# How a two-layer mixer trunk begins its first layer: four column blocks over four row tiles instead of three over six

## The chip, the cores and the metric

The kernel runs on one core of a Trainium2 chip. The metric is the device time of one execution in microseconds (us). TensorE is called PE here, its weight loads PEld, VectorE DVE, ScalarE ACT, GpSimd POOL and SyncE SP.

## What is computed

Two layers of a residual stream x of 256 rows and 2048 channels. Each layer normalizes x, projects it by one wide matrix, runs a convolution branch and a latent-attention branch on parts of the projection, merges both by gates, projects the result and adds it to x. Cut to the part that matters here:

```python
def hybrid_layer(x, ...):
    h = rmsnorm(x, norm_g)
    proj = h @ w_in                      # 2048 x 13376
    (c_a, c_glu, c_gate, q_down, kv_down, k_pe, m_gate,
     g_conv, g_mla) = jnp.split(proj, idx, axis=-1)
    y_conv = conv_branch(c_a, c_glu, c_gate, ...) @ w_proj_conv
    y_mla = mla_branch(q_down, kv_down, k_pe, m_gate, cos, sin, ...) @ w_proj_mla
    y = jax.nn.sigmoid(g_conv) * y_conv + jax.nn.sigmoid(g_mla) * y_mla
    return x + y @ w_out
```

The convolution's input is `c_a * sigmoid(c_glu)`. q_down, kv_down and k_pe, 512 + 512 + 64 columns, are the narrow ("down") projections from which queries, keys and values are made.

## The kernel before, in words

**Products.** Every matrix product is done in float32 accuracy from two halves. A weight w is split into hi (w rounded to PE's fp32r type, by an ACT cast) and lo = w - hi (by a DVE subtraction); the activations likewise into h_hi and h_lo. Three products are summed in PSUM: h_hi x hi, h_lo x hi and h_hi x lo. The stationary operand is a 128 x 128 tile of the activations, the weights move past it.

**Pieces.** Weights come from HBM in pieces: two K tiles (row tiles of 128 channels) of one block of n columns (512, 384 or 320), so 128 x 2n numbers. A piece needs 12 products: 2 K tiles x 2 row blocks of 128 rows (t = 0, 1) x 3 halves. Eight pieces make one block of a 2048-channel product. Pieces are numbered in the order in which PE takes them; "piece 10" below is the eleventh. For each piece, SP issues the load (`load`), ACT casts hi (`split_hi`), DVE subtracts lo (`split_lo`), and PE multiplies. SP loads 4 pieces ahead of the cast, the cast is issued 3 pieces ahead of PE and the subtraction 2 (`LOAD_AHEAD`, `HI_AHEAD`, `LO_AHEAD`). There are 5 raw buffers, 4 for hi, 3 for lo; a load waits for the lo of the piece 5 before it.

**Order.** On each engine instructions run in the order in which the program issues them (`InOrder`), so a wait holds up all that stands behind it. `background` counts slots, one after each piece, and at each slot issues steps that are due (`at_slot`): evacuations of PSUM, loads, the steps of other parts of the layer.

**The first layer's begin.** x arrives transposed, K tile by K tile (`load_x`; tile 0 comes with the gains in `gx`). `first_h` makes h_hi and h_lo of one K tile, on ACT (tile 0: DVE) and DVE. It stands just before the cast of the first piece that reads those K tiles (`h_of`). The rows of x are loaded again untransposed (`xres`) to sum their squares on ACT (`first_sums`, `sum_x`); the factor `rinv_x` that normalizes rows is first needed when a block is evacuated. So that PE does not need a new K tile with every piece, `plan_first` (line 211) and `products_together` (line 419) take several blocks together: here the first gated unit ("unit 0", 512 columns, `glu`) and the first two down blocks of 384 columns, over the first 3 pieces (6 K tiles) each, by turns; after that the rest of unit 0 (5 pieces), of down block 0 and of down block 1. Down block 2, of 320 columns, follows by itself (`product`, line 385), then `down_after` (line 692) starts the steps for the keys and queries. The blocks that are open at the same time stand in different PSUM homes: `acc0`, `acc1`, `s`, `tp`.

**The very first piece** is loaded, cast and subtracted by K tile, and not as a whole (`SINGLE = 1`, lines 258 and 268), and its products run K tile by K tile. Ahead of them `N_WARM = 19` products on zeros (line 580) warm PE while the loads come. The loads at the start are written out by hand:

```python
    act.dma_start(gx, g_in)
    load_x(act, 1, 2)
    ...
    load(0)
    load(1)
    load(2)
    load_x(sp, 2, 4)
    load(3)
    load(4)
    load_x(sp, 4, 6)
    at_slot(1, lambda: load_x(sp, 6, 8))
    at_slot(3, lambda: load_x(sp, 8, 12))
    at_slot(5, lambda: load_x(sp, 12, 16))
```

Of the kernel before, what the change touches and what calls it, by code (L numbers as in the profile page):

```python
# [57 lines left out]
R_QA, R_KVA, R_QR, R_KR, R_N = 0, LORA, 2 * LORA, 2 * LORA + ROPE, 2 * LORA + 2 * ROPE  # L58

KS = 2  # L60
SINGLE = 1
FIRST_TOGETHER, FIRST_DOWNS = 3, (2, 1)
TOGETHER = (("pconv", 0), ("wout", 0))
N_WARM = 19

# [64 lines left out]
def trunk(ctx: ExitStack, tc: tile.TileContext, xT, x, g_in, pos, win, wuq, wukv, wpc, wpm, wo, cst, rows, invf, out):  # L132
# [78 lines left out]
    def plan_first(layer, stream):  # L211

        ap, nk = streams[stream]
        count, groups = 1 + FIRST_DOWNS[layer], nk // KS
        widths = blocks_of_layer()[stream][:count]
        starts = [nk * P * sum(widths[:i]) for i in range(count)]
        if layer == 0:
            joint, rest = range(FIRST_TOGETHER), range(FIRST_TOGETHER, groups)
            order = [(i, g) for g in joint for i in range(count)] + [(i, g) for i in range(count) for g in rest]
        else:  # L220
            order = [(i, g) for part in (range(6), range(6, groups)) for i in range(count) for g in part]
        mine = []
        for i, g in order:
            n = widths[i]
            size = P * KS * n
            at = starts[i] + g * size
            pieces.append((ap[layer, at : at + size].rearrange("(p e) -> p e", p=P), n))
            mine.append((i, g, len(pieces) - 1))
            if i == 0 and layer == 0:
                h_of[len(pieces) - 1] = range(g * KS, (g + 1) * KS)  # L230
        taken[layer, stream] = (count, nk * P * sum(widths))
        return nk, widths, mine
# [20 lines left out]
    def load(i):  # L253
        if i >= len(pieces) or i in loaded:
            return
        ap, n = pieces[i]
        loaded[i] = t = raw_p.tile([P, KS * n], F32, tag="raw", name=f"raw{i}")
        for a in range(0, KS, 1 if i < SINGLE else KS):
            k = slice(a, a + 1 if i < SINGLE else KS)
            sp.dma_start(part_of(i, t, k), part_of(i, ap, k))  # L260

    def split_hi(i):
        if i >= len(pieces) or i in highs:
            return
        load(i)
        highs[i] = split_p.tile([P, KS * pieces[i][1]], F32R, tag="hi", name=f"hi{i}", bufs=4)
        singly = i < SINGLE
        for a in range(0, KS, 1 if singly else KS):
            k = slice(a, a + 1 if singly else KS)

            for step in ("h", "w"):
                if step == "w":
                    act.copy(part_of(i, highs[i], k), part_of(i, loaded[i], k))
                    if singly:
                        split_lo(i, k)
                else:
                    for c in h_of.get(i, ())[k.start : k.stop]:
                        first_h(c)
        for a in range(1, LOAD_AHEAD + 1):
            load(i + a)  # L280

# [69 lines left out]
    def order_of_products(i, last):  # L351

        two = range(2)
        if i < SINGLE:
            return [(t, kk, p) for kk in range(KS) for p in range(3) for t in two]
        high, low = (lambda t, p: [(t, kk, p) for kk in range(KS)]), (lambda t: [(t, kk, 2) for kk in range(KS)])
        if last:
            return high(0, 0) + high(0, 1) + high(1, 0) + low(0) + high(1, 1) + low(1)  # L360
        return [e for t in two for p in two for e in high(t, p)] + low(0) + low(1)
# [54 lines left out]
                steps.insert(0, (clock[0] + 1 + evac_at, costs, evac))  # L416
            background(n)

    def products_together(planned, stat, evacuate, evac_at, costs, before=None):

        nk, widths, mine = planned
        pts = []
        for i in range(2):
            blocks_begun[0] += 1
            tags = [f"acc{blocks_begun[0] % 2}{t}" for t in range(T)]
            pts.append([acc_p.tile([P, 512], F32, tag=tag, name=f"acc{mine[0][2]}_{i}{t}") for t, tag in enumerate(tags)])
        if len(evac_at) == 3:
            pts.insert(0, [s_p.tile([P, 512], F32, tag=f"s{t}", name=f"acc{mine[0][2]}_s{t}") for t in range(T)])
        if len(evac_at) == 4:
            both = tp_p.tile([P, T, 512], F32, tag="tp", name=f"acc{mine[0][2]}_tp")  # L430
            pts[1:1] = [
                [s_p.tile([P, 512], F32, tag=f"s{t}", name=f"acc{mine[0][2]}_s{t}") for t in range(T)],
                [both[:, t] for t in range(T)],
            ]
        ends = nk // KS - 1

        def evac(i):
            for t in range(T):
                evacuate(i, t, pts[i][t][:, : widths[i]])

        for i, g, piece in mine:
            n = widths[i]
            for a in range(HI_AHEAD + 1):
                split_hi(piece + a)
                if a <= LO_AHEAD:
                    split_lo(piece + a)
            hi, lo, _ = done[piece]
            if before and i == 0:
                before(g)
            for t, kk, part in order_of_products(piece, g == ends):  # L450
                k = g * KS + kk
                sh, sl = stat(k, t)
                stationary, w = ((sh, hi), (sl, hi), (sh, lo))[part]
                pe.matmul(
                    pts[i][t][:, :n], stationary, woven(piece, w, kk),
                    start=k == 0 and part == 0, stop=k == nk - 1 and part == 2,
                )
            if g == ends:
                steps.insert(0, (clock[0] + 1 + evac_at[i], costs[i] if isinstance(costs[0], tuple) else costs, lambda i=i: evac(i)))
            background(n)  # L460
# [103 lines left out]
    act.dma_start(gx, g_in)  # L564
    load_x(act, 1, 2)
    act.copy(sin2[:, 0, 0, :], ones[:, :HALF].bitcast(F32))
    load(0)
    load(1)
    load(2)
    load_x(sp, 2, 4)  # L570
    load(3)
    load(4)
    load_x(sp, 4, 6)
    at_slot(1, lambda: load_x(sp, 6, 8))
    at_slot(3, lambda: load_x(sp, 8, 12))
    at_slot(5, lambda: load_x(sp, 12, 16))


    warm = tp_p.tile([P, 256], F32, tag="tp", name="warm")
# [85 lines left out]
    for l in range(DEPTH):  # L665
# [783 lines left out]
        for kind, i, pl in planned:  # L1449
            if kind == "glu":  # L1450
                at = 0 if i in (2, 5) else EVAC_AT
                if i == 0 and l == 0:
                    at = 6 - 2 * FIRST_TOGETHER
                    for n, (t, c) in enumerate([(0, 0), (0, 2), (1, 0), (1, 2)]):
                        begin, end = first_sums(t, c)
                        at_slot((4, 5, 6, 9)[n], begin)
                        at_slot((9, 9, 10, 12)[n], end, 0.0, 1.5)
                    at_slot(13, sum_x, 2.2)
                elif i == 0:
                    at_slot(8, sum_x, 2.2)  # L1460
                if i == 0:
                    at_slot(10, load_consts)
                if i == 0:
                    if l == 0:
                        rope_table_steps()
                    downs = FIRST_DOWNS[l]
                    products_together(
                        pl, uses_h, lambda i, t, ps: down_evac(i - 1, t, ps) if i else glu_evac(0, t, ps),
                        (at,) + downs * (EVAC_AT,), ((0.9, 2.2),) + downs * ((0.0, 1.0),),
                    )  # L1470
                    continue
                product(pl, uses_h, lambda t, ps, i=i: glu_evac(i, t, ps), at, (0.9, 2.2))
            elif kind == "down":
# [26 lines left out]
            elif kind == "cgate":  # L1500
                product(pl, uses_h, lambda t, ps, i=i: cgate_evac(i, t, ps), costs=(0.0, 2.0))
            elif kind == "pconv":
                while "yc" not in keep:
                    run_fill()
                products_together(pl, stat_of(*keep["yc"]), pconv_evac, (EVAC_AT, EVAC_AT, EVAC_AT, 0), (2.4, 0.0), before_pconv)
            elif i == 0:
                wout_begin(0)
                wout_begin(1)
                products_together(pl, stat_of(*keep["y"]), wout_evac, (EVAC_AT, EVAC_AT), (1.25, 1.5))
            else:  # L1510
                at_slot(3, lambda i=i: wout_begin(i))
                product(pl, stat_of(*keep["y"]), lambda t, ps, i=i, f=wout_evac: f(i, t, ps),
                        0 if i == 3 else EVAC_AT, (1.25, 1.5),
                        final=last_half if last_layer and i == 3 else None)
# [43 lines left out]
def _layout(inp):  # L1558
# [33 lines left out]
    rows_of_w = {"wuq": _rows()[:LORA], "wukv": _rows()[:LORA]}  # L1592
    g = np.stack([f("norm_g")[l][rows_of[l]] for l in range(DEPTH)])
    win = np.stack([_blocked(f("w_in")[l][rows_of[l]][:, cols], bl["win"]) for l in range(DEPTH)])
    first = win[0, : SINGLE * P * KS * bl["win"][0]].reshape(SINGLE, P, 2, KS, -1)
    first[...] = first.transpose(0, 1, 3, 2, 4).copy().reshape(first.shape)
    return {
        "xT": np.ascontiguousarray(x.reshape(SEQ, NCT, P).transpose(2, 1, 0)),
        "x": x.reshape(T, P, D),
# [29 lines left out]
```

## Time and profile before

| | |
|---|---|
| median of 3 runs | 1785.10 us (1784.71 to 1785.26) |
| profiled execution: its own time | 1785.14 us |
| profiled execution: span of the trace | 1783.4 us |
| busy in the span: PE, PEld, DVE, ACT, POOL | 1777.9, 1572.1, 1537.7, 1293.8, 550.4 us |
| moved by DMA | 463.65 MB, mean 260 GB/s |

The span runs from the first instruction to the last. Each engine's busy time is the union of its instructions, so 100% for PE says that it had hardly any gap, not that each product was as short as it can be.

### The profile page before, as it was taken

Reading aid. Unit: us, or ns where it says so; the run is one execution under the profiler, and the core shown is the slowest. Engines: PE = TensorE matmul, PEld = TensorE weight load, DVE = VectorE, ACT = ScalarE, POOL = GpSimd, SP = SyncE. Lnnn points to the kernel's source line nnn. Section 1 sums busy time; section 2 is a strip of 40 time slices with the busy share of each in tenths; the row PEclk is TensorE's granted clock in tenths of the full one; section 3 lists DMA queues with packets and bytes.
Section 4 is the critical chain, followed back from the end, with each engine's and each line's share of the span. In section 5 each row is a group of like instructions: output and inputs, shape, how many; then the busy total and the mean of one; then the engine's idle time right before and its main releaser. Section 6 shows DMA issues by size and latency. Waiting matters only on the chain.

```text
span 1783.4 us, 27086 instructions
## 1 busy us (share of the span) xinstructions
PE 1777.9 (100%) x8577; PEld 1572.1 (88%) x8577; DVE 1537.7 (86%) x2485; ACT 1293.8 (73%) x2397; POOL 550.4 (31%) x1009
## 2 busy tenths in 40 slices
PE   9999999999999999999999999999999999999999
PEld 9988888888888888888899888888888888888887
DVE  6899899898999998867669898989999999887674
ACT  7679889888877675744567698898888777666442
POOL 0055556642311110021421555566333111100210
PEclk9999999999999999999999999999999999999999
DMA  9787888887989986678977888788879899866785
GB/s 334 242 277 256 279 268 275 273 290 235 281 247 254 268 247 231 220 245 285 314 259 229 261 286 269 255 285 275 286 238 279 244 254 262 257 210 220 247 281 179
DMA packets 149375, 463.65 MB, mean 260 GB/s; under 512 B 24816, under 2 KB 30704, under 8 KB 149232
## 3 DMA queue, kind: packets, MB, share of 16 engines
q1 hardware_dynamic: 105712, 360.42, 61.5%
q0 software_dynamic: 42928, 100.98, 20.2%
q8 instruction: 67, 1.10, 0.3%
q14 instruction: 76, 0.62, 0.1%
q10 hardware_dynamic: 592, 0.54, 0.1%
HBM read 399.18 MB, written 44.04 MB: 249 GB/s over the span
## 4 chain that ended last, share of the span: by engine, by line
PE 99%; DMA 1%; DVE 0%; ACT 0%; issue 0%; DVEq 0%; ACTq 0%
PE acc L143 90%; PE acc_s L143 4%; PE acc_tp L143 2%; PE s L143 2%; PE o_ps L143 1%; DMA raw<-in_win 1%; DVE xres L143 0%; DVE u_t L143 0%; ACT hi L143 0%; DVE qkc L143 0%; DVE su L143 0%; PE var L143 0%; ACT su L143 0%; PE mu L143 0%; DVEq L143 0%
## 5 line engine op out<-in xcount | busy, mean ns | idle before, releaser
L143 ACT CAST hi<-raw 128x1024 fp32r<-128x1024 f32 (+2 forms) x681 | 693.5, 1028 | 369.5 <-PE acc L143 229.8
L143 DVE TENSOR_TENSOR lo<-raw,hi 128x1024 fp32r<-128x1024 f32 (+2 forms) x681 | 812.0, 1195 | 144.7 <-PE acc L143 79.1
L143 PE MATMUL acc<-hi,hT 128*128 128x512 f32 (+2 forms) x1728 | 400.8, 372 | 0.2 <-DVE su L143 0.2
L143 PEld LDWEIGHTS acc<-hi,hT 128*128 128x128 f32 x1728 | 319.7, 189 | 40.9 <-PE acc L143 0.4
L143 DVE SCALAR_TENSOR_TENSOR v_t<-u_t,cst,v_t 128x256 f32<-128x256 f32 x562 | 239.9, 479 | 2.1
L143 PE MATMUL acc<-hi,h_hi 128*128 128x512 f32 (+2 forms) x832 | 241.5, 372 | 0.0
L143 PE MATMUL acc<-hi,h_lo 128*128 128x512 f32 (+2 forms) x832 | 241.5, 372 | 0.0
L143 PE MATMUL acc<-lo,hT 128*128 128x512 f32 (+2 forms) x864 | 220.1, 372 | 0.0
L143 PE MATMUL acc<-lo,h_hi 128*128 128x512 f32 (+2 forms) x832 | 211.8, 372 | 0.0
L143 PEld LDWEIGHTS acc<-lo,hT 128*128 128x128 f32 x864 | 160.8, 189 | 20.6
L143 PEld LDWEIGHTS acc<-hi,h_lo 128*128 128x128 f32 x832 | 155.5, 189 | 19.8
L143 PEld LDWEIGHTS acc<-lo,h_hi 128*128 128x128 f32 x832 | 154.8, 189 | 19.7
L143 PEld LDWEIGHTS acc<-hi,h_hi 128*128 128x128 f32 x832 | 154.6, 189 | 19.2
L143 POOL DMA_DIRECT2D turn_d<-gate x176 | 95.8, 553 | 217.6 <-DVE gate L143 151.9
L143 POOL DMA_DIRECT2D taps<-taps x71 | 62.1, 875 | 299.4 <-ACT taps L143 219.4
L143 ACT ACTIVATE taps<-u_t,cst 128x256 f32<-128x256 f32 x292 | 128.4, 498 | 2.9 <-DVE v_t L143 2.2
L143 PE MATMUL acc<-hi,oT 128*128 128x512 f32 x512 | 122.2, 379 | 0.0
L143 PE MATMUL acc<-hi,yT 128*128 128x512 f32 x512 | 122.0, 378 | 0.0
L143 POOL DMA_DIRECT2D turned<-turn_d x88 | 50.0, 578 | 217.1 <-ACT hi L143 59.9
L143 PE MATMUL acc<-hi,qkc 128*128 128x512 f32 x448 | 110.8, 380 | 0.1
L143 PEld LDWEIGHTS acc<-hi,oT 128*128 128x128 f32 x512 | 96.8, 189 | 13.7
L143 PEld LDWEIGHTS acc<-hi,yT 128*128 128x128 f32 x512 | 96.6, 189 | 13.6
(197 smaller groups left out, 2428.1 us busy)
## 6 DMA issues: line engine op xcount, KB each, us to landing
raw<-in_win SPq DMA_DIRECT2D x383, 512.0 KB, 4.6
raw<-in_wpm SPq DMA_DIRECT2D x64, 512.0 KB, 5.0
raw<-in_wpc SPq DMA_DIRECT2D x64, 512.0 KB, 4.3
raw<-in_wo SPq DMA_DIRECT2D x64, 512.0 KB, 5.2
taps<-taps POOLq DMA_DIRECT2D x71, 256.0 KB, 6.5
raw<-in_wukv SPq DMA_DIRECT2D x32, 512.0 KB, 4.4
turned<-turn_d POOLq DMA_DIRECT2D x56, 256.0 KB, 5.6
raw<-in_win SPq DMA_DIRECT2D x32, 384.0 KB, 5.1
```

The source lines that it names most:

```text
L143: ins = getattr(self.engine, name)(*a, **k)
```

## The change

Unit 0 and all three down blocks start together, over the first 2 pieces (4 K tiles) each, in the order down block 2 (320 columns), down block 0 (384), unit 0 (512), down block 1 (384). The four open blocks stand in `s` (unit 0), two `acc` homes and `tp` (down block 2). The two smallest first pieces are loaded, cast and subtracted by K tile and by turns, and their 24 products run together, K tile by K tile; piece 1 then has none left. Behind the joint part come the rest of unit 0 (6 pieces) and of each down block (6 pieces each). `down_after` is called behind the joint product. x tiles 4 to 15 are loaded at slots 2, 3, 5 and 7, where tiles 4 and 5 stood among the first loads and the others at slots 1, 3 and 5. There are 17 warming products. The second layer's parameters stay as they were.

```diff
-SINGLE = 1
-FIRST_TOGETHER, FIRST_DOWNS = 3, (2, 1)
+SINGLE = 2
+FIRST_TOGETHER, FIRST_ORDER, FIRST_DOWNS = 2, (3, 1, 0, 2), (3, 1)
-N_WARM = 19
+N_WARM = 17
...
-            order = [(i, g) for g in joint for i in range(count)] + [(i, g) for i in range(count) for g in rest]
+            order = [(i, g) for g in joint for i in FIRST_ORDER] + [(i, g) for i in range(count) for g in rest]
...
-            if i == 0 and layer == 0:
+            if layer == 0 and i == (FIRST_ORDER[0] if g in joint else 0):
                 h_of[len(pieces) - 1] = range(g * KS, (g + 1) * KS)
...
+    def load_singles():
+        for i in range(SINGLE):
+            loaded[i] = raw_p.tile([P, KS * pieces[i][1]], F32, tag="raw", name=f"raw{i}")
+        for kk in range(KS):
+            for i in range(SINGLE):
+                k = slice(kk, kk + 1)
+                sp.dma_start(part_of(i, loaded[i], k), part_of(i, pieces[i][0], k))
+
+    def split_singles():
+        for i in range(SINGLE):
+            high_tile(i)
+        for kk in range(KS):
+            k = slice(kk, kk + 1)
+            first_h(kk)
+            for i in range(SINGLE):
+                act.copy(part_of(i, highs[i], k), part_of(i, loaded[i], k))
+            for i in range(SINGLE):
+                split_lo(i, k)
...
-            for t, kk, part in order_of_products(piece, g == ends):
+            todo = [(piece, i) + e for e in order_of_products(piece, g == ends)]
+            if piece < SINGLE:
+                first = [(q, j) for j, _, q in mine[:SINGLE]]
+                todo = [(q, j, t, kk, p) for kk in range(KS) for p in range(3) for q, j in first for t in range(T)] if piece == 0 else []
+            for q, j, t, kk, part in todo:
...
-    load(0)
-    load(1)
+    load_singles()
     load(2)
+    load(3)
     load_x(sp, 2, 4)
-    load(3)
     load(4)
-    load_x(sp, 4, 6)
-    at_slot(1, lambda: load_x(sp, 6, 8))
-    at_slot(3, lambda: load_x(sp, 8, 12))
-    at_slot(5, lambda: load_x(sp, 12, 16))
+    for slot, (a, b) in ((2, (4, 6)), (3, (6, 8)), (5, (8, 12)), (7, (12, 16))):
+        at_slot(slot, lambda a=a, b=b: load_x(sp, a, b))
...
-                    at = 6 - 2 * FIRST_TOGETHER
+                    at = 6 - 3 * FIRST_TOGETHER
...
+                        homes=("acc", "acc") if l else ("s", "acc", "acc", "tp"),
                     )
+                    if downs == len(DOWN_BLOCKS):
+                        down_after()
                     continue
```

PE's first rows in the kernel before (acc_s is the home of unit 0; the numbers behind hi, lo and raw are buffer numbers, one per piece; the size is that of the output):

```order
L143 MATMUL warm<-const-float32-0.0 128x256 x19
L143 MATMUL acc_s_163<-hi_165,h_hi 128x512
L143 MATMUL acc_s_164<-hi_165,h_hi 128x512
L143 MATMUL acc_s_163<-hi_165,h_lo 128x512
L143 MATMUL acc_s_164<-hi_165,h_lo 128x512
L143 MATMUL acc_s_163<-lo_169,h_hi 128x512
```

and now (acc_3 is down block 2 in `tp`, acc_10 and acc_11 are down block 0):

```order
L143 MATMUL warm<-const-float32-0.0 128x256 x17
L143 MATMUL acc_3_163<-hi_164,h_hi 128x320 x2
L143 MATMUL acc_10_159<-hi_165,h_hi 128x384
L143 MATMUL acc_11_160<-hi_165,h_hi 128x384
L143 MATMUL acc_3_163<-hi_164,h_lo 128x320 x2
L143 MATMUL acc_10_159<-hi_165,h_lo 128x384
L143 MATMUL acc_11_160<-hi_165,h_lo 128x384
```

The first products are narrower, and each pair of one block is followed by a pair of the other, which needs a load of its own.

SP's queue in the kernel before, from the load of piece 7 (raw_212 is piece 8, raw_230 piece 9, raw_253 piece 10, raw_275 piece 11, raw_298 piece 12; the x_in row of 512 columns is x tiles 6 and 7, those of 1024 are x tiles 8 to 11 and 12 to 15):

```order
L143 DMA raw_193<-in_win 128x768
L143 DMA x_in<-in_xT 128x512
L143 DMA raw_212<-in_win 128x768
L143 DMA raw_230<-in_win 128x1024
L143 DMA x_in<-in_xT 128x1024
L143 DMA raw_253<-in_win 128x1024
L143 DMA xres<-in_x 128x512 x2
L143 DMA raw_275<-in_win 128x1024
L143 DMA x_in<-in_xT 128x1024
L143 DMA xres<-in_x 128x512 x2
L143 DMA raw_298<-in_win 128x1024
```

and now (raw_231 is piece 9, raw_250 piece 10, raw_272 piece 11, raw_299 piece 12, raw_325 piece 13; the x_in rows of 512 columns are x tiles 4 and 5, 6 and 7):

```order
L143 DMA x_in<-in_xT 128x512
L143 DMA raw_231<-in_win 128x1024
L143 DMA x_in<-in_xT 128x512
L143 DMA raw_250<-in_win 128x1024
L143 DMA xres<-in_x 128x512 x2
L143 DMA raw_272<-in_win 128x1024
L143 DMA x_in<-in_xT 128x1024
L143 DMA xres<-in_x 128x512 x2
L143 DMA raw_299<-in_win 128x1024
L143 DMA xres<-in_x 128x512 x2
L143 DMA raw_325<-in_win 128x1024
L143 DMA x_in<-in_xT 128x1024
```

x tiles 8 to 11 moved from ahead of piece 10 to behind piece 11, x tiles 12 to 15 from ahead of piece 12 to behind piece 13.

ACT's order now, from the h_hi of K tiles 8 and 9 (hi_346 is piece 10, hi_435 piece 13; junk is a square of x's rows for the sums):

```order
L143 ACTIVATE h_hi<-x_in,gx 128x256 x2
L143 CAST hi_346<-raw_250 128x1024
L143 ACTIVATE h_hi<-x_in,gx 128x256 x2
L143 CAST hi_368<-raw_272 128x1024
L143 ACTIVATE junk,ss_x<-xres 128x512 x4
L143 ACTIVATE h_hi<-x_in,gx 128x256 x2
L143 CAST hi_402<-raw_299 128x1024
L143 ACTIVATE junk,ss_x<-xres 128x512 x2
L143 ACTIVATE h_hi<-x_in,gx 128x256 x2
L143 CAST hi_435<-raw_325 128x1024
```

From piece 10 on the kinds and the order of ACT's rows are those of before (there hi_340 is piece 10 and hi_428 piece 13).

## Rows read from the trace of the kernel before

**Rows 1.** The page: busy us and shares by engine; the chain that ended last
```profile
PE 1777.9 (100%) x8577; PEld 1572.1 (88%) x8577; DVE 1537.7 (86%) x2485; ACT 1293.8 (73%) x2397; POOL 550.4 (31%) x1009
...
PE 99%; DMA 1%; DVE 0%; ACT 0%; issue 0%; DVEq 0%; ACTq 0%
```

**Rows 2.** PE's waits, whole span: waited for, us in total, times, longest
```profile
PE warm L143 <- PEq L1618: 0.8, 1, 0.8
PE acc_s L143 <- ACT hi L143: 0.3, 1, 0.3
PE acc L143 <- DVE su L143: 0.2, 1, 0.2
```

**Rows 3.** The chain in order of time: start us, us, what, instructions
```profile
8.41 3.90 PE acc L143 x24
...
25.29 12.95 PE acc_s L143 x60
```

**Rows 4.** Timeline 0 to 9 us: start, us, engine, operation, [idle before, releaser]
```profile
0.78 4.18 PE L143 MATMUL warm<-const-float32-0.0 128*128 128x256 f32 x19 [0.78 <-PEq L1618]
...
4.60 0.62 ACT L143 CAST hi<-raw 128x512 fp32r<-128x512 f32 x1 [1.41 <-DMA raw<-in_win]
...
4.78 0.35 DVE L143 TENSOR_SCALAR h_hi<-gx 128x256 fp32r<-128x256 f32 x1 [3.77 <-DMA gx<-in_g]
...
5.27 0.70 PE L143 MATMUL acc_s<-hi,h_hi 128*128 128x512 f32 x2 [0.31 <-ACT hi L143]
...
5.77 0.51 ACT L143 ACTIVATE h_hi<-x_in,gx 128x256 fp32r<-128x256 f32 x1 [0.55 <-DMA x_in<-in_xT]
...
6.84 0.70 PE L143 MATMUL acc_s<-hi,h_hi 128*128 128x512 f32 x2
7.38 0.59 PE L143 MATMUL acc_s<-hi,h_lo 128*128 128x512 f32 x2
...
8.24 0.49 PE L143 MATMUL acc<-hi,h_hi 128*128 128x384 f32 x2
```

**Rows 5.** Timeline 18 to 35 us, ACT, and SP's issue of piece 13
```profile
21.97 1.05 ACT L143 CAST hi<-raw 128x1024 fp32r<-128x1024 f32 x1 [0.88 <-DMA raw<-in_win]
...
23.48 0.33 SPq L143 DMA_DIRECT2D raw<-in_win  x1
...
24.81 1.04 ACT L143 CAST hi<-raw 128x1024 fp32r<-128x1024 f32 x1 [0.97 <-DMA raw<-in_win]
...
28.64 0.89 ACT L143 ACTIVATE h_hi<-x_in,gx 128x256 fp32r<-128x256 f32 x2
29.44 1.03 ACT L143 CAST hi<-raw 128x1024 fp32r<-128x1024 f32 x1
...
32.55 1.03 ACT L143 CAST hi<-raw 128x1024 fp32r<-128x1024 f32 x1
```

**Rows 6.** DMA issues from 23.4 to 24 us: KB each, median us to landing
```profile
raw<-in_win SPq DMA_DIRECT2D x1, 512.0 KB, 7.8
```

**Rows 7.** Stretches: length, busy us by engine, PEclk, DMA share, GB/s
```profile
4.00:8.00 4.00, 3.69 (x17) 2.71 (x17) 3.06 (x6) 2.70 (x5) 0.00 (x0) 1.00 1.00 368
16.00:19.00 3.00, 3.00 (x20) 2.97 (x19) 1.62 (x3) 1.68 (x5) 0.00 (x0) 1.00 0.95 342
19.00:22.00 3.00, 3.00 (x17) 2.71 (x16) 2.16 (x4) 1.98 (x4) 0.00 (x0) 1.00 0.95 301
22.00:38.00 16.00, 16.00 (x81) 14.42 (x80) 11.73 (x27) 14.02 (x29) 0.00 (x0) 1.00 1.04 401
```

**Rows 8.** Timeline 38 to 58 us, ACT, DVE and PE
```profile
38.35 1.28 ACT L143 ACT_TABLE_LOAD   x1 [1.19 <-DVE rinv_x L143]
...
40.94 0.95 DVE L143 TENSOR_TENSOR lo<-raw,hi 128x768 fp32r<-128x768 f32 x1
...
43.27 0.81 PE L143 MATMUL acc<-lo,h_hi 128*128 128x384 f32 x4
...
51.27 0.73 ACT L143 CAST hi<-raw 128x640 fp32r<-128x640 f32 x1 [1.07 <-PE acc L143]
```

More of the change, by code (lines that the diff above doesn't have):

```diff
@@ L257, in load, with high_tile @@
         loaded[i] = t = raw_p.tile([P, KS * n], F32, tag="raw", name=f"raw{i}")
-        for a in range(0, KS, 1 if i < SINGLE else KS):
-            k = slice(a, a + 1 if i < SINGLE else KS)
-            sp.dma_start(part_of(i, t, k), part_of(i, ap, k))
+        sp.dma_start(t, ap)
+    def load_singles():
[5 more added lines that the diff above has]
+                sp.dma_start(part_of(i, loaded[i], k), part_of(i, pieces[i][0], k))
+    def high_tile(i):
+        highs[i] = split_p.tile([P, KS * pieces[i][1]], F32R, tag="hi", name=f"hi{i}", bufs=4)
+        return highs[i]
+    def split_singles():
[8 more added lines that the diff above has]
+                split_lo(i, k)
     def split_hi(i):
@@ L265, in split_hi @@
         load(i)
[L266 to L278, printed above, removed]
+        if i < SINGLE:
+            split_singles()
+        else:
+            for c in h_of.get(i, ()):
+                first_h(c)
+            act.copy(high_tile(i), loaded[i])
         for a in range(1, LOAD_AHEAD + 1):
@@ L355, in order_of_products @@
         two = range(2)
-        if i < SINGLE:
-            return [(t, kk, p) for kk in range(KS) for p in range(3) for t in two]
         high, low = (lambda t, p: [(t, kk, p) for kk in range(KS)]), (lambda t: [(t, kk, 2) for kk in range(KS)])
@@ L417, in product, with products_together @@
             background(n)
-    def products_together(planned, stat, evacuate, evac_at, costs, before=None):
+    def products_together(planned, stat, evacuate, evac_at, costs, before=None, homes=("acc", "acc")):
         nk, widths, mine = planned
         pts = []
[L423 to L434, printed above, removed]
+        for i, home in enumerate(homes):
+            if home == "tp":
+                both = tp_p.tile([P, T, 512], F32, tag="tp", name=f"acc{mine[0][2]}_{i}")
+                pts.append([both[:, t] for t in range(T)])
+                continue
+            blocks_begun[0] += home == "acc"
+            pool, tag = (acc_p, f"acc{blocks_begun[0] % 2}") if home == "acc" else (s_p, "s")
+            pts.append([pool.tile([P, 512], F32, tag=f"{tag}{t}", name=f"acc{mine[0][2]}_{i}{t}") for t in range(T)])
         ends = nk // KS - 1
@@ L446, in products_together @@
                     split_lo(piece + a)
-            hi, lo, _ = done[piece]
             if before and i == 0:
                 before(g)
-            for t, kk, part in order_of_products(piece, g == ends):
+            todo = [(piece, i) + e for e in order_of_products(piece, g == ends)]
[3 more added lines that the diff above has]
+            for q, j, t, kk, part in todo:
                 k = g * KS + kk
                 sh, sl = stat(k, t)
-                stationary, w = ((sh, hi), (sl, hi), (sh, lo))[part]
+                stationary, w = ((sh, done[q][0]), (sl, done[q][0]), (sh, done[q][1]))[part]
                 pe.matmul(
-                    pts[i][t][:, :n], stationary, woven(piece, w, kk),
+                    pts[j][t][:, : widths[j]], stationary, woven(q, w, kk),
                     start=k == 0 and part == 0, stop=k == nk - 1 and part == 2,
@@ L1504, in trunk @@
                     run_fill()
-                products_together(pl, stat_of(*keep["yc"]), pconv_evac, (EVAC_AT, EVAC_AT, EVAC_AT, 0), (2.4, 0.0), before_pconv)
+                products_together(pl, stat_of(*keep["yc"]), pconv_evac, (EVAC_AT, EVAC_AT, EVAC_AT, 0), (2.4, 0.0), before_pconv, ("acc", "s", "tp", "acc"))
             elif i == 0:
@@ L1594, in _layout @@
     win = np.stack([_blocked(f("w_in")[l][rows_of[l]][:, cols], bl["win"]) for l in range(DEPTH)])
-    first = win[0, : SINGLE * P * KS * bl["win"][0]].reshape(SINGLE, P, 2, KS, -1)
-    first[...] = first.transpose(0, 1, 3, 2, 4).copy().reshape(first.shape)
+    for b in FIRST_ORDER[:SINGLE]:
+        at = NCT * P * sum(bl["win"][:b])
+        first = win[0, at : at + P * KS * bl["win"][b]].reshape(P, 2, KS, -1)
+        first[...] = first.transpose(0, 2, 1, 3).copy().reshape(first.shape)
     return {
```

## The prediction

> **What bounds the kernel now.** Read the busy shares and the chain first: TensorE (PE) is busy for 1777.9 of 1783.4 us, and 99% of the chain that ended last is PE [rows 1]. Then PE's own waits, over the whole run: 0.8 us before the first warming product, 0.3 us before the first real product, 0.2 us once in the second layer [rows 2]. So only two things can move the end: when the first real product starts, and whether a wait comes in afterwards. Everything that the change touches lies in the first 45 us, so I keep one number through the text, the **lag**: the time on the clock less the work that PE has done by then. Products follow each other at 12.95/60 = 0.2158 us for 512 columns and 3.90/24 = 0.1625 us for 384 [rows 3]; on the same line, 320 columns would take 0.136 us (an estimate). In the kernel before, the first piece (12 products of 512 columns, 2.59 us of work) ends at 8.24 [rows 4]: a lag of 5.65 us. It is 4.96 us of warming, 0.31 us until the first product, and 0.38 us because the piece took 2.97 instead of 2.59 us: its pairs at 5.27 and 6.84 take 0.70 us where PE runs on 0.59 us would do, about 0.1 us for each wait that breaks the stream. After 8.24 PE never waits in this stretch, so 5.65 us stays to the end.
>
> What feeds PE there is a queue. The raw casts of ScalarE (ACT) at 21.97 and 24.81 each begin when a load lands, after 0.88 and 0.97 us of idling [rows 5], while the DMA engines are full and move 401 GB/s between 22 and 38 us (392 of the KB in which sizes are given, per us), 368 between 4 and 8, but only 342 and 301 GB/s between 16 and 22 us [rows 7]. Loads are thus late by bytes, in the order in which SP issues them.
>
> **The head.** Two warming products less free 2 x 0.22 us (4.18/19) [rows 4], so PE is free at 4.52; that alone decides nothing, because the first product waits for data. In before, gx and the first half piece (144 + 256 KB) share the engines; gx opens DVE's first step at 4.78, the half piece opens ACT's cast at 4.60 [rows 4]. Now the half piece is 160 KB, 96 KB less, at 368 GB/s 0.27 us: gx lands at 4.49, h_hi is there at 4.49 + 0.02 + 0.35 = 4.86, the cast of 320 columns (0.62 us for 512 [rows 4] and 1.05 for 1024 [rows 5], so an estimated 0.46) ends before that, and PE starts at about 4.95. The next product, for down block 0, needs its own half piece. In before the second x tile, which opens ACT at 5.77, had 784 KB with and before it; now 624 KB, 0.45 us less: 5.30, and the half piece lands between 5.1 and 5.3. Its cast of 384 columns (0.51) ends by 5.75, PE goes on at 5.8, when it would have been through the first pair at 5.22. The other 22 of the 24 joint products are 3.31 us, with 0.1 for the break they end at 9.2. Their work is 3.58 us: lag 5.62, **a gain of 0.03 us**. Bounds: no wait for the second half piece, a gain of 0.6; the half piece 0.3 us later than taken, a loss of 0.27. I take the middle, as its loads are the same bytes on the same queue.
>
> **The loads behind it.** Bytes are the same in sum; what moves is the place of x tiles 8 to 11 and 12 to 15. Before, the queue up to and with the raw load of piece 11 holds 7440 KB and that piece's cast starts at 24.81 [rows 5]. Now the queue up to and with x tiles 8 to 11 holds 7312 KB, because 512 KB of x rows for the sums and piece 11 itself went ahead of them: 128 KB less, 0.33 us, so they land at **24.46**. In before they stood ahead of piece 10, whose cast starts at 21.97. X tiles 12 to 15 are now behind piece 13, 9872 KB into the queue; in before piece 13, issued at 23.48, lands 7.8 us later, at 31.28, with 10000 KB [rows 5, 6]. So they land at **30.95**; before, they stood between pieces 11 and 12.
>
> The Trainium skill, "DMA: Bandwidth & Descriptors", Specifications, gives a limit of about 358 GB/s of HBM for one core. The rows between 22 and 38 us (401) contradict it; by it the 2560 KB between the two x loads would take 7.3 instead of 6.5 us, and the sum below would be about 2.6 us.
>
> **The chain on ACT.** ACT works in order, and x 8 to 11 now hold up everything after them. From 24.48 come two h_hi (0.80, from 28.64 to 29.44 in before, the cast after them starting there), the cast of piece 10 (1.05, less the 0.1 by which ACT starts its next step before an end: 0.95), two h_hi (0.80): the cast of piece 11 starts at 27.03, 2.22 us later than its 24.81 [rows 5]. From there ACT's order is the same as before: four squares for the sums, h_hi 12 and 13, cast 12, two squares, h_hi 14 and 15, cast 13. The h_hi at 28.64 [rows 5] moves to 30.86, but x lands at 30.95: 30.97, 2.33 us late. Cast 13, from 32.55 to 33.58 in before, ends at **35.91**. Behind it the same chain follows as before, without slack: two squares, the sum and reciprocal root on DVE, for which ACT idles 1.19 us ahead of its table load at 38.35, the evacuation of the first unit, and then on DVE the low half of piece 16, 0.95 us from 40.94 to 41.89 [rows 8]. All is 2.33 us later: 44.22.
>
> **The sum.** PE reaches piece 16's low products in before at 43.27 [rows 8], 1.38 us after their data. The work ahead of them was 3 x 6.49 + 5 x 2.59 + 2 x 1.95 + 1.30 = 37.62 us, lag 5.65. Now two joint groups of 1600 columns (8.12 each), six pieces of the unit, two of a down block and 8 products: 36.98 us. With lag 5.62 PE would be there at 42.60; the data come at 44.22, PE goes on at 44.27 and loses 0.1 on the break: lag 44.37 - 36.98 = 7.39, **1.74 us more than before**. This contains the waits on the way (piece 12 for cast 12, at 32.80; piece 13 for cast 13, at 35.91), since the latest one sets the lag. The early start is swallowed. Behind piece 16 the order is as in before, where ACT waits for PE again, 1.07 us ahead of its cast at 51.27 [rows 8], so nothing should be added, and no other PE work changes: the number of real products and their columns is the same. Evacuating the last block from another PSUM home and starting the key and query steps after the joint product moves no work onto PE; 16 pieces of 512 columns (16 x 2.59 = 41 us of PE) lie between them and the first product that reads their result, and I cost it at nothing; without that cover it would cost what those steps come late.
>
> The profiled execution took 1785.14 us against a median of 1785.10, so the sum stands on either: 1785.14 + 1.74 = **1786.9 us**.
>
> **Rivals.**
> *The engines run full.* Nothing in the code makes 16 to 22 us slow. If those 6 us ran at 401 GB/s, (59 + 100) GB/s x 3 us = 477 thousand bytes more would move, 1.19 us. All landings and the chain come that much earlier: low half 16 at 43.03, lag 43.18 - 36.98 = 6.20, 0.55 more than before: 1785.7. With slack in the chain as well, and no wait in the head, the gain of 0.6 stays: 1784.5. For it: the dip is one stretch of one execution. Against: three runs agree within 0.55 us, so it likely recurs, and x rows for the sums are read there in both kernels.
> *The clock comes late.* The warming products take 0.22 us for 256 columns, the 1.2 GHz level; from 5.27 on 512 columns take 0.2158, the 2.4 GHz level [rows 3, 4]. With 19 products it rose before the first real one, at most 4.5 us after the start. Now PE idles from 4.52, perhaps ahead of the rise. If the lower level lasts 4.5 us beyond the first product, half of that is lost: lag 7.87, which takes the place of the load wait: 1787.4. Twice as long loses 4.5 us: 1789.6. It makes the kernel slower by over 0.2% once the lower level lasts more than 7.2 us after the first product. Against: real products fill PE soon after, and the 0.31 us of idling in before did no harm.
> The Trainium skill, "TensorE: Matmul & The Clock Gate", Part 1, says that the rise follows from time spent active and not from a number of products, and that its moment varies from run to run. By that rule two products less may or may not be enough; before's warming row agrees only in that all but its end runs at the lower level.
> *The change does not do what it says:* the joint start gives no earlier product because half pieces now queue one behind the other. That is inside the head's bounds, 0.27 us lost at most, and does not decide.
>
> **How the numbers follow.** A measurement of this kernel can tell 0.2%, 3.6 us, from no change. X tiles late, lag up by 1.1 to 2.6 us (1786.2 to 1787.7): 0.58. Engines full, or slack where I see none (1784.5 to 1786.2): 0.28. Clock late: 0.06, of which 0.03 beyond 0.2%. Left over, anything else in the pipeline: 0.08. The range is 1784.6 to 1787.7. Within 0.2% holds nearly all of the first two and half of the clock: 0.95; slower 0.04, faster 0.01.
>
> **What would show it.** Right: PE waits for ACT at 32 to 36 us and for DVE's low half at 44, together near 1.7 us; ACT idle from about 20 until an h_hi near 24.5, released by x_in; the first real product near 4.95 and a wait inside the first pair. Wrong: no PE wait after 10 us (then x came in time and the lag is below 5.65), x 8 to 11 landing before 23.3, or products at half pace after 5 us.

## The result, and the profile after

The changed kernel takes 1787.98 us (median of 22 executions, 1787.19 to 1789.05), the kernel before 1785.09 us on the same chip (22 executions, 1784.51 to 1786.21). The ratio is 1.0015 with an interval of [1.0009, 1.0022]: slower by 2.9 us, inside the 0.2% that was called no change, and outside the forecast range of 1784.6 to 1787.7 by 0.3 us. The profiled execution took 1787.63 us at a span of 1785.9 us; its increase over the profiled execution of before is 2.5 us. One of the eleven executions of run 5 below took 2684.9 us, at a granted clock of 0.65, and is left out of its ratio.

The page of the kernel after, its busy shares (against [rows 1]):

```profile
PE 1778.5 (100%) x8575; PEld 1575.0 (88%) x8575; DVE 1537.2 (86%) x2486; ACT 1295.0 (73%) x2398; POOL 556.2 (31%) x1009
```

Of the 2.5 us by which the span is longer, PE idles for 1.9 us and is busy for 0.6 us more (1778.5 against 1777.9 us, with two products fewer, the warming ones); the last section shows that a wait also lengthens the busy rows beside it. The view of PE's waits over the whole span of after, in the columns of [rows 2]:

```profile
PE acc L143 <- ACT hi L143: 1.7, 3, 1.1
PE warm L143 <- PEq L1631: 0.8, 1, 0.8
PE acc L143 <- DVE su L143: 0.4, 1, 0.4
PE acc L143 <- DVE lo L143: 0.2, 1, 0.2
```

Three waits for ACT's raw casts and one for a low half on DVE are new. The wait for DVE's su was there before with 0.2 us and lies in the second layer; in the ten profiles it takes from nothing to 0.8 us. Where the four new ones stand shows in the timeline of PE in after, with its first 8 us (columns as in [rows 4]):

```profile
0.78 3.91 PE L143 MATMUL warm<-const-float32-0.0 128*128 128x256 f32 x17 [0.78 <-PEq L1631]
4.79 0.97 PE L143 MATMUL acc<-hi,h_hi 128*128 128x320 f32 x4
5.60 0.76 PE L143 MATMUL acc<-hi,h_lo 128*128 128x320 f32 x4
6.20 0.76 PE L143 MATMUL acc<-lo,h_hi 128*128 128x320 f32 x4
6.80 0.85 PE L143 MATMUL acc<-hi,h_hi 128*128 128x320 f32 x4
...
27.33 0.70 PE L143 MATMUL acc<-hi,h_hi 128*128 128x512 f32 x2 [0.32 <-ACT hi L143]
...
33.87 0.70 PE L143 MATMUL acc<-hi,h_hi 128*128 128x512 f32 x2 [1.09 <-ACT hi L143]
...
36.98 0.70 PE L143 MATMUL acc<-hi,h_hi 128*128 128x512 f32 x2 [0.26 <-ACT hi L143]
...
45.29 0.92 PE L143 MATMUL acc<-lo,h_hi 128*128 128x384 f32 x4 [0.25 <-DVE lo L143]
```

A row's form is that of its first product: each x4 at the start is two products of 320 columns and two of 384. From 6.20 to 6.80 these four take 0.60 us, and at the 2.4 GHz pitch they take 2 x 0.136 + 2 x 0.1625 = 0.60: PE ran at the upper level. The waits belong to piece 10, piece 12, piece 13 and the low half of piece 16. In lag: 5.43 us after the joint pieces (5.65 in before), 6.02 after the wait at 27.33, 7.37 after 33.87, 7.90 after 36.98, and 8.42 after 45.29, which is **2.77 us more than before**; at the end the span is 2.5 us longer. The lag is read from one execution, and what comes after it differs from execution to execution: the span of run 6 below is 4.0 us above before's with a lag only 2.56 us larger, as its second layer holds one more wait of 1.1 us (for DVE's qk_t) and 0.7 us for su.

What ACT waited for, in its timeline of after (against [rows 5, 8]):

```profile
17.78 0.91 ACT L143 ACTIVATE h_hi<-x_in,gx 128x256 fp32r<-128x256 f32 x2 [2.35 <-DMA x_in<-in_xT]
...
25.43 0.91 ACT L143 ACTIVATE h_hi<-x_in,gx 128x256 fp32r<-128x256 f32 x2 [3.87 <-DMA x_in<-in_xT]
26.25 1.03 ACT L143 CAST hi<-raw 128x1024 fp32r<-128x1024 f32 x1
27.18 0.91 ACT L143 ACTIVATE h_hi<-x_in,gx 128x256 fp32r<-128x256 f32 x2
27.99 1.03 ACT L143 CAST hi<-raw 128x1024 fp32r<-128x1024 f32 x1
28.93 0.63 ACT L143 ACTIVATE junk<-xres 128x512 f32<-128x512 f32 x1
...
31.98 0.91 ACT L143 ACTIVATE h_hi<-x_in,gx 128x256 fp32r<-128x256 f32 x2
32.79 1.03 ACT L143 CAST hi<-raw 128x1024 fp32r<-128x1024 f32 x1
...
35.90 1.76 ACT L143 CAST hi<-raw 128x1024 fp32r<-128x1024 f32 x2
...
41.69 1.28 ACT L143 ACT_TABLE_LOAD   x1 [1.19 <-DVE rinv_x L143]
```

ACT idles 3.87 us until x tiles 8 to 11 land at 25.41; then it works without a break: two h_hi, cast of piece 10, two h_hi, cast 11, squares from 28.93. X tiles 12 to 15 land at 31.95 and open the h_hi at 31.98; cast 12 follows at 32.79 and cast 13 at 35.90, and PE's waits at 33.87 and 36.98 end with those two casts. After the squares and the same 1.19 us of idling as in before, the table load stands at 41.69 instead of 38.35. The last link is in DVE's timeline of after:

```profile
39.08 0.16 DVE L143 TENSOR_REDUCE totx<-ss_x 128x2 f32<-128x8 f32 x1
...
43.49 0.88 DVE L143 SCALAR_TENSOR_TENSOR su<-acc,rinv_x,su 128x256 f32<-128x256 f32 x2 [0.97 <-ACT su L143]
44.28 2.69 DVE L143 TENSOR_TENSOR lo<-raw,hi 128x768 fp32r<-128x768 f32 x3
```

The sum of x's squares is finished at 39.24, the first unit is evacuated at 43.49, and only then comes piece 16's low half, which PE uses at 45.29.

Last, the stretches of the loads, after and then before (columns as in [rows 7]):

```profile
11.00:17.00 6.00, 6.00 (x40) 5.92 (x39) 4.56 (x6) 2.75 (x4) 0.00 (x0) 1.00 0.94 273
17.00:23.00 6.00, 6.00 (x33) 5.53 (x32) 4.06 (x6) 3.69 (x6) 0.00 (x0) 1.00 1.03 402
...
22.00:31.00 9.00, 8.68 (x41) 7.29 (x40) 4.87 (x7) 5.50 (x12) 0.00 (x0) 1.00 1.04 406
```
```profile
11.00:17.00 6.00, 6.00 (x35) 5.68 (x34) 5.12 (x7) 4.55 (x8) 0.00 (x0) 1.00 1.03 384
17.00:23.00 6.00, 6.00 (x35) 5.68 (x34) 4.17 (x6) 4.32 (x8) 0.00 (x0) 1.00 0.96 334
```

Both kernels have a slow stretch while their DMA engines are busy (shares of 0.94 to 0.96). In before it lies behind 15 us; in after it lies at 11 to 17 us and is deeper, 273 GB/s over 6 us.

### The profile page after: what moved, and what is told of

It reads as the page before. It is cut to its first block, busy times and chain, and to the rows that moved or that the text cites. A ratio compares the mean times of both kernels' runs of the same rounds, so it can differ in the third digit from the quotient of the medians.

```text
span 1785.9 us, 27083 instructions
## 1 busy us (share of the span) xinstructions
PE 1778.5 (100%) x8575; PEld 1575.0 (88%) x8575; DVE 1537.2 (86%) x2486; ACT 1295.0 (73%) x2398; POOL 556.2 (31%) x1009
## 4 chain that ended last, share of the span: by engine, by line
PE 97%; DMA 2%; DVE 0%; ACT 0%; issue 0%; SPq 0%; DVEq 0%; ACTq 0%
PE acc L143 94%; PE s L143 2%; DMA raw<-in_win 1%; PE o_ps L143 1%; DMA x_in<-in_xT 0%; DMA pos_t<-in_pos 0%; DVE lo L143 0%; ACT hi L143 0%; SPq L143 0%; DVE rsq_t L143 0%; DVE xres L143 0%; DVE su L143 0%; ACT su L143 0%; DVE rinv_x L143 0%; PE var L143 0%
## 5 line engine op out<-in xcount | busy, mean ns | idle before, releaser
L143 ACT CAST hi<-raw 128x1024 fp32r<-128x1024 f32 (+3 forms) x682 | 694.6, 1027 | 376.2 <-PE acc L143 291.2
L143 DVE TENSOR_TENSOR lo<-raw,hi 128x1024 fp32r<-128x1024 f32 (+3 forms) x682 | 812.3, 1194 | 145.7 <-PE acc L143 107.4
L143 PE MATMUL acc<-hi,h_hi 128*128 128x512 f32 (+2 forms) x864 | 251.5, 373 | 1.8 <-ACT hi L143 1.7
L143 PE MATMUL acc<-hi,h_lo 128*128 128x512 f32 (+2 forms) x864 | 250.9, 373 | 0.0
L143 PE MATMUL acc<-lo,h_hi 128*128 128x512 f32 (+2 forms) x864 | 220.3, 373 | 0.2 <-DVE lo L143 0.2
L143 PEld LDWEIGHTS acc<-hi,h_hi 128*128 128x128 f32 x864 | 160.5, 190 | 23.2 <-ACT hi L143 3.2
L143 PEld LDWEIGHTS acc<-hi,h_lo 128*128 128x128 f32 x864 | 161.8, 189 | 20.2
L143 PEld LDWEIGHTS acc<-lo,h_hi 128*128 128x128 f32 x864 | 161.1, 189 | 20.8 <-DVE lo L143 0.5
L143 PE MATMUL acc<-hi,ycT 128*128 128x512 f32 x512 | 122.3, 379 | 0.0
```

The lines of the kernel that those rows point to most:

```text
L143: ins = getattr(self.engine, name)(*a, **k)
```

## The experiments

Two theories. **Late x:** the whole loss is that x tiles 8 to 11 and 12 to 15 are loaded behind two more pieces each, by the chain on ACT of the prediction. **Rivals:** the shorter warming and the joint start cost something of their own; or the bound is the chain from the squares to piece 16's low half, whenever x comes. All ratios are to the kernel before, run on the same chip.

**1. The x loads back at their old slots, the rest of the change kept.**

```diff
-    for slot, (a, b) in ((2, (4, 6)), (3, (6, 8)), (5, (8, 12)), (7, (12, 16))):
+    for slot, (a, b) in ((2, (4, 6)), (3, (6, 8)), (3, (8, 12)), (5, (12, 16))):
```

> The changed kernel with x tiles 8 to 11 and 12 to 15 loaded at slots 3 and 5, as before the change, nothing else. Theory (these two loads came too late): both land some 4 to 5 us earlier (about 21 and 27 us), PE's waits for hi of pieces 10, 12 and 13 go, at most 0.3 us is left at the low half of piece 16, the lag stays at 5.4 to 5.9 us, and the time comes back to 1784.7 to 1785.5 us. Rival (four blocks over two pieces each ask for bytes faster than the engines bring them, wherever x stands): piece loads that now stand behind x come late instead, PE still waits for ACT's casts around 25 to 37 us, time 1787 us or more.

Measured: 1784.85 us, ratio 0.9999 [0.999, 1.0008]. X 8 to 11 land at 21.04, 12 to 15 at 26.22; lag after piece 16 5.31. The view of PE's waits of this kernel:

```profile
PE warm L143 <- PEq L1631: 0.8, 1, 0.8
PE acc L143 <- DVE su L143: 0.4, 1, 0.4
PE acc L143 <- ACT hi L143: 0.3, 1, 0.3
```

The one wait for ACT that is left is at 5.25, inside the first joint pair: the wait for down block 0's half piece that the prediction put there, in this execution. The waits for ACT and for the low half behind 10 us are gone from the view, and with them the loss (the wait for su lies in the second layer, and after has it too). So late x is shown to be the cause. The chain to piece 16's low half still has no slack here: these products start at 42.19, 0.05 us behind their data, and the break costs 0.15 us of the lag (5.16 to 5.31). The version is the best one here, but its 0.05 us below before's 1784.9, and the 0.34 us of lag by which it is ahead, are both far inside the interval: it beats before by nothing that could be measured.

**2. The same late x in the kernel before, nothing else of the change.**

```diff
-    at_slot(3, lambda: load_x(sp, 8, 12))
-    at_slot(5, lambda: load_x(sp, 12, 16))
+    at_slot(5, lambda: load_x(sp, 8, 12))
+    at_slot(7, lambda: load_x(sp, 12, 16))
```

> The kernel before with x tiles 8 to 11 and 12 to 15 loaded at slots 5 and 7, as the change does, nothing else. Theory: the queue up to them holds 7440 and 10000 KB, they land at 24.8 to 25.8 and 31.3 to 32.3 us, the cast of piece 13 ends at 36.2 or later, the low half of piece 16 at 44.5 or later; lag 7.1 to 8.1 where before has 5.65: 1786.5 to 1787.6 us. Rival (the joint start of four blocks makes the loss): no wait comes in, 1785.1 us as before.

Measured: 1786.56 us, ratio 1.0007 [0.9999, 1.0016], landings at 25.16 and 32.03, lag 7.85 (2.2 us more than before). The timeline of PE in this kernel:

```profile
5.15 1.19 PE L143 MATMUL acc_s<-hi,h_hi 128*128 128x512 f32 x2
...
33.95 0.70 PE L143 MATMUL acc_s<-hi,h_hi 128*128 128x512 f32 x2 [0.79 <-ACT hi L143]
...
37.06 0.70 PE L143 MATMUL acc_s<-hi,h_hi 128*128 128x512 f32 x2 [0.26 <-ACT hi L143]
...
45.37 0.92 PE L143 MATMUL acc<-lo,h_hi 128*128 128x384 f32 x4 [0.25 <-DVE lo L143]
```

The last three waits of after come up in a kernel that has neither the joint start nor the shorter warming, within 0.1 us of the same places. The interval reaches just below 1, so the time alone does not show it; the trace does. Late x alone thus brings 2.2 of after's 2.77 us of lag. The other 0.6 us come of late x and the new order of pieces together: the low half of piece 16 is there at the same time within 0.1 us, but PE does 37.62 us of work before it in this order and 36.98 in after's, so after has less work done when that wait ends.

The row at 5.15 shows something else: the two products of 512 columns there take 0.98 us until the next row, at 6.13, where 0.43 would do at 2.4 GHz and 0.85 at 1.2. In this execution PE was still at the lower level when its real products began, with 19 warming products.

**3. Nineteen warming products in the changed kernel.**

```diff
-N_WARM = 17
+N_WARM = 19
```

> The changed kernel with 19 warming products. Theory: the first product starts 0.2 to 0.4 us later than the changed kernel's 4.79, but the waits at pieces 12, 13 and 16 end when their data are there, so the time is the changed kernel's own within 0.3 us: 1787.6 to 1788.3. Rival (the clock or the head matters): another time by 0.5 us or more in either direction.

Measured: 1788.13 us, ratio 1.0018 [1.0009, 1.0026]; first product at 4.68 instead of 4.79, lag 8.66, landings at 25.66 and 32.20. The first product came 0.11 us earlier, where 0.2 to 0.4 us later was forecast. The number of warming products changes nothing in the time that could be measured.

**4. The squares for the sums later, in the changed kernel.**

```diff
-                        at_slot((4, 5, 6, 9)[n], begin)
-                        at_slot((9, 9, 10, 12)[n], end, 0.0, 1.5)
+                        at_slot((6, 7, 8, 10)[n], begin)
+                        at_slot((10, 11, 12, 13)[n], end, 0.0, 1.5)
```

> The changed kernel with the x rows for the sums loaded at slots 6, 7, 8, 10 and squared at slots 10 to 13, where they were at 4, 5, 6, 9 and 9, 9, 10, 12. x tiles 8 to 11 then have 512 KB less ahead of them (1.3 us), 12 to 15 have 1024 KB less (2.6 us). Theory (the last wait sets the lag, and that is the chain squares, row factor, evacuation, low half of piece 16): PE no longer waits at piece 13, but the last square comes about 1 us later than the changed kernel's 39.05, the low half of piece 16 ends near 46.3, lag near 9.4: 1788.5 to 1789.5 us. Rival (x tiles alone are the cause): waits go, 1785.0 to 1786.0 us.

Measured: 1789.47 us (9 executions, 1787.36 to 1791.97), ratio 1.0026 [1.0016, 1.0036]; the profiled execution is one of the two shortest, 1787.51 us. X lands earlier, at 23.77 and 28.99, since x's rows for the sums no longer stand ahead of it, and no wait for ACT is left; but the lag is 8.91 (9.4 was forecast). The view of PE's waits, and the timeline of PE, of this kernel:

```profile
PE acc L143 <- DVE lo L143: 2.4, 2, 1.8
```
```profile
4.85 1.77 PE L143 MATMUL acc<-hi,h_hi 128*128 128x320 f32 x4
6.41 0.96 PE L143 MATMUL acc<-hi,h_lo 128*128 128x320 f32 x4
7.21 0.76 PE L143 MATMUL acc<-lo,h_hi 128*128 128x320 f32 x4
...
43.04 0.92 PE L143 MATMUL acc<-lo,h_hi 128*128 128x384 f32 x4 [1.84 <-DVE lo L143]
...
45.79 0.92 PE L143 MATMUL acc<-lo,h_hi 128*128 128x384 f32 x4 [0.53 <-DVE lo L143]
```

The squares now end later (the sum starts at 39.58 instead of 39.08), the unit's evacuation with them. On DVE the low half of piece 15 waits behind the steps of the sum and that of piece 16 behind the evacuation. This edit is no remedy, but it shows the chain of the second rival by itself: it binds here although PE no longer waits for ACT. Run 1 has the same chain without slack, and only takes away what made it late.

The first three rows are the head: the four products from 4.85 to 6.41 take 1.56 us, where 0.60 would do at 2.4 GHz and 1.20 at 1.2. PE was at the lower level here too, with 17 warming products, and the eight products up to 7.21 took 1.17 us longer than the upper level needs. The waits behind them swallowed that.

**5 and 6. One of the two x loads back, the other left late.**

```diff
-    for slot, (a, b) in ((2, (4, 6)), (3, (6, 8)), (5, (8, 12)), (7, (12, 16))):
+    for slot, (a, b) in ((2, (4, 6)), (3, (6, 8)), (3, (8, 12)), (7, (12, 16))):
```

> The changed kernel with x tiles 8 to 11 alone back at slot 3; 12 to 15 stay at slot 7. Theory (two limits side by side: ACT's chain from x 8 to 11, and the landing of x 12 to 15, each late by itself): x 8 to 11 land near 21, the wait at piece 10 goes, but the h_hi of K tile 12 still waits for x 12 to 15 near 32, the casts of pieces 12 and 13 end at 33.8 and 36.9 as in the changed kernel, lag about 8.4: 1787.3 to 1788.3 us. Rival (x 8 to 11 alone are late, the rest only follows): 1785 to 1785.8 us.

```diff
-    for slot, (a, b) in ((2, (4, 6)), (3, (6, 8)), (5, (8, 12)), (7, (12, 16))):
+    for slot, (a, b) in ((2, (4, 6)), (3, (6, 8)), (5, (8, 12)), (5, (12, 16))):
```

> The changed kernel with x tiles 12 to 15 alone back at slot 5, right behind 8 to 11, which stay. Theory: x 12 to 15 land near 27, but ACT still starts K tile 8 near 25.4 and reaches the h_hi of K tile 12 near 31.9, where it was at 31.98; casts 12 and 13 within 0.2 us of the changed kernel's, lag 8.2 to 8.4: 1787.2 to 1788.2 us. Rival (x 12 to 15 alone are late): 1785 to 1785.8 us.

Measured: with x 8 to 11 back 1788.11 us, 1.0015 [1.0006, 1.0024], lag 7.62 (about 8.4 was forecast), landings 20.69 and 31.15. With x 12 to 15 back 1787.91 us, 1.0013 [1.0004, 1.0022], lag 8.21, landings 25.38 and 26.67. Waits of PE in the timeline, in the first and in the second:

```profile
33.07 0.70 PE L143 MATMUL acc<-hi,h_hi 128*128 128x512 f32 x2 [0.93 <-ACT hi L143]
...
36.18 0.70 PE L143 MATMUL acc<-hi,h_hi 128*128 128x512 f32 x2 [0.26 <-ACT hi L143]
```
```profile
33.66 0.70 PE L143 MATMUL acc<-hi,h_hi 128*128 128x512 f32 x2 [0.92 <-ACT hi L143]
...
36.77 0.70 PE L143 MATMUL acc<-hi,h_hi 128*128 128x512 f32 x2 [0.26 <-ACT hi L143]
```

Undoing either half alone gives back 0.8 or 0.2 us of lag (two executions of after, below in run 7, differ by 0.4) and nothing measurable in time; undoing both gives 3.1. The two loads are two limits side by side on ACT's ordered queue: with x 8 to 11 in time ACT stops for x 12 to 15 (2.52 us of idling before the h_hi at 31.18), and with x 12 to 15 in time ACT still gets x 8 to 11 over 4 us later than in run 5. The prediction had them as two links with 0.1 us between them (30.86 against 30.95); measured are 0.20 (ACT is ready for the h_hi at 31.78 in run 6, and it starts at 31.98 in after). That is why neither helps by itself.

**7 and 8. After and before once more, unchanged, for the spread of the landings.** No edit.

> The changed kernel itself, for a second profile and the time on this chip. Theory (the stretch in which the engines move less than 400 GB/s differs from one execution to the next and sets how late x lands): x 8 to 11 land at another time between 24.4 and 26, and the lag after piece 16 moves with that landing one for one; median 1787.3 to 1788.3 us. Rival (the stretch is a fixed part of this order of loads): the same landing, 25.4, within 0.1 us.

> The kernel before itself, for a second profile. Theory: a stretch of slow loads comes again between 10 and 22 us, of another size than the 1.2 us in the first profile; x 12 to 15 land within 1 us of 26; no PE wait comes of it, 1784.5 to 1785.6 us. Rival (the stretch was one accident): 390 GB/s or more throughout from 8 to 22 us.

Measured: after 1787.73 us, 1.0013 [1.0004, 1.0022], landings 25.82 and 32.35, lag 8.81; before 1785.04 us, landings 20.86 and 26.11, lag 5.60. Between the two executions of after, x lands 0.41 us later and the lag is 0.39 us larger: one for one, as the theory had it. Before has its slow stretch again, so it was no accident of one execution. GB/s by the stretches of all ten profiles, with the landing of x tiles 8 to 11 (24.46 us is when the prediction had them land):

| kernel | 11 to 17 us | 15 to 22 us | 22 to 31 us | 0 to 24.46 us | x 8 to 11 |
|---|---|---|---|---|---|
| before / again | 384 / 371 | 332 / 327 | 408 / 405 | 332 / 333 | 20.16 / 20.86 |
| 2 (before, x late) | 372 | 321 | 405 | 330 | 25.16 |
| after / again | 273 / 292 | 353 / 339 | 406 / 406 | 321 / 317 | 25.41 / 25.82 |
| 3 (19 warming) | 298 | 363 | 405 | 318 | 25.66 |
| 6 (x 12 to 15 back) | 285 | 332 | 407 | 318 | 25.38 |
| 1, 4, 5 | 310, 310, 316 | 373, 383, 388 | 404, 400, 402 | 333, 331, 330 | 21.04, 23.77, 20.69 |

The three profiles with before's start are slowest at 15 to 22 us, the seven with the joint start at 11 to 17 us, and all ten move 400 to 408 GB/s between 22 and 31 us. The joint start moves the stretch, but it does not by itself cost bytes: up to 24.46 us runs 1, 4 and 5, with the same start, have moved as much as before. Of the seven, only the four with x tiles 8 to 11 behind piece 11 and the sums' rows (after, its repeat, runs 3 and 6) are behind, by 3 to 5%.

## Why the prediction missed its range

- **The mechanism held.** The loss is x tiles 8 to 11 and 12 to 15 landing late and holding up ACT's ordered queue; the early start is swallowed. Run 1 takes the late x away and the loss is gone, run 2 puts it alone into the kernel before and 2.2 us of lag come up.
- **The chain on ACT held to 0.02 us.** From the landing of x 12 to 15 the prediction had 4.96 us to the end of cast 13 and 13.27 us to piece 16's low half. Measured from 31.95: cast 13 ends at 36.93 (4.98), the low half is there at 45.24 (13.29).
- **The step that failed is in the loads behind the head: x tiles 8 to 11 at 24.46, x 12 to 15 at 30.95.** They land at 25.41 and 31.95, 0.95 and 1.00 us later, and those 1.0 us are the miss in lag: 1.74 us forecast, 2.77 us measured. I took the landing by bytes from before's curve, with its slow stretch as [rows 7] show it, and argued about that stretch in one direction only, that it might not be there (the rival that fills the engines). It came, earlier and deeper. That it would be deeper in this order of loads than in before's was nowhere in the sum or the rivals. From 0 to 24.46 us before moves 8.12 MB and after 7.86 MB by the stretches: 0.26 MB less, 0.65 us at 401 GB/s. The other 0.3 us are what is left over: at 25.41, when x 8 to 11 are complete, after has moved 0.13 MB more than before had at 24.46. That loads issued behind x had moved a part of theirs by then would explain it; it is not shown.
- **The rate behind the slow stretch held.** The two x loads land 6.54 us apart, forecast 6.49. The Trainium skill, "DMA: Bandwidth & Descriptors", Specifications, would make that 7.3 us by its limit of about 358 GB/s for one core; this trace contradicts it again with 402 to 406 GB/s. The sum that went by that page, 2.6 us, is near the measured one, but not for its reason.
- **The head** was better than forecast: the first product at 4.79 (4.95 forecast) and, in this execution, no wait of note inside the first pair, for a lag of 5.43 instead of 5.62 us. In run 1 a wait was there: 0.34 us, up to 5.25, where 5.22 to 5.8 was forecast. Both are inside the bounds given, and both are swallowed by the later waits.
- **A wait at piece 10** (27.33) was not forecast. It is the same late x, 0.95 us later than taken, and lies ahead of larger waits, so it adds nothing of its own.
- **The clock rival** did not happen in the profiled execution of after, whose rows at 5.60 and 6.20 go at the 2.4 GHz pitch, so it has no part in these 2.77 us. In runs 2 and 4, with 19 and 17 warming products, the first real products go at the lower level, and in run 5, with 17, the first three do. Run 4, where this lasts until about 6.8, loses 1.17 us over its first eight products; after loses 0.22 there. The prediction priced a rise 4.5 us after the first product (2.25 us lost, 0.06); it came sooner than that in all ten profiles, and the waits behind the head set the lag. In run 1, with 17, PE was at the upper level in its first joint pair. The Trainium skill, "TensorE: Matmul & The Clock Gate", Part 1, has the rise follow from time and not from a number of products, and its moment vary from run to run. These runs agree, with either level under 17 and under 19 warming products.
- **Moving the evacuation and starting key and query steps later** was costed at nothing. Run 1 has both, and its whole time is before's (1784.85 against 1784.90 us): it agrees.

## What to carry to other kernels

A load that is put behind others in a full queue is late by bytes, but the rate at which those bytes move was not the old kernel's here: its slow stretch came earlier and deeper when the order of the loads changed. A curve taken from the old trace has to be carried with an uncertainty in both directions. Where an engine works in order and the chain behind it has no slack, a late operand shifts all that follows one for one; here the chain read off the old trace held to 0.02 us. Before undoing one of two late loads, see how much slack lies between them: here it was 0.1 to 0.2 us, and only undoing both paid.

## What was not expected of the hardware

**Loads have a slow stretch early in the program, in every profile.** With the DMA engines nearly as busy as later (shares of 0.92 to 1.00 against 1.03 to 1.04), 6 to 7 us run at 273 to 332 GB/s, against 400 to 408 between 22 and 31 us. In after's trace 207 of the 242 packets of 4096 bytes from 11 to 17 us take 0.159 us and 11 take 1.2 to 1.9 us; from 22 to 31 us none takes over 0.18 us. In before's stretch, 15 to 22 us, only 2 of 398 take over 1 us. The place goes with the order of the first loads, 15 to 22 us with before's start and 11 to 17 with the joint one. Why some packets stall stays open; another placement of the data in memory was not tried.

**A break in PE's stream costs more than the wait that is shown.** In after, the wait at 27.33 shows 0.32 us of idling and adds 0.59 us of lag: 0.16 us because PE without a break starts a product that long before the row of the one ahead of it ends (that row ends at 27.01, and the next product would have started at 26.85), and 0.10 us because the second product follows the first after 0.320 instead of 0.216 us. About the same 0.27 us beyond the wait shown come with each of the other three (1.35 for 1.09, 0.53 for 0.26, 0.52 for 0.25).
